# Background steps of a layer's FFN: issued by GpSimd through two buffers, one step at every hook, and spilled weight pairs as one transfer

## The chip, the cores and the metric

The kernel runs on one core of a Trainium2 chip. The metric is the device time of one execution in microseconds (us), lower is better. The engines of the core are named TensorE (PE; its weight loads are shown apart as PEld), VectorE (DVE), ScalarE (ACT), GpSimd (POOL) and SyncE (SP). SyncE and GpSimd can both start DMA transfers between the chip's main memory and the on-chip memory; each has a queue that it works off in order.

## What is computed

The reference is a trunk of two layers over a sequence of 1024 positions and 1024 channels, in fp32. Each layer has a token mixing and an FFN, both modulated by a vector `c`:

```python
for l in range(DEPTH):                       # DEPTH = 2
    mod = c_act @ w_ada[l] + b_ada[l]        # six vectors of 1024
    sh1, sc1, gt1, sh2, sc2, gt2 = jnp.split(mod, N_MOD, axis=-1)
    h = modulate(rms_norm(x, g_mix[l]), sh1, sc1)
    p = h @ w_in[l]                          # three head groups: Fourier, recurrence, attention
    ...
    x = x + gt1[:, None, :] * y
    h = modulate(rms_norm(x, g_ffn[l]), sh2, sc2)
    f = (silu(h @ w_ffn_gate[l]) * (h @ w_ffn_up[l])) @ w_ffn_down[l]   # 2816 inner channels
    x = x + gt2[:, None, :] * f
```

The change touches two things that layer 1 needs and that are made ready during layer 0's FFN: the products `c_act @ w_ada[1]`, and copies of layer 1's first weights.

## The kernel before

**Products.** A weight or an activation `w` is split into `hi` (rounded to the type that TensorE takes) and `lo = w - hi`, and every product is three matmuls, hi.hi, hi.lo and lo.hi (`mm3`). `split` makes the pair: ScalarE copies hi (line 199), VectorE subtracts (line 202). Nearly all operations are recorded at the line of their helper: 191 matmul, 199 activation, 202 tensor_tensor, 205 scalar_tensor_tensor.

**The FFN loop.** The 2816 inner channels are 22 blocks of 128, f = 0 to 21 (the first two run differently). For f from 2 on there are seven jobs (`p_job`, line 1363), each one operand of a fast scheme of products with 12 matmuls and half a weight; `after` (line 1399) takes their results from PSUM, applies silu and the product, and `a_split` writes the block's activations as a hi/lo pair into `ffa_A` (even f) or `ffb_A` (odd f), two halves each; the down weights go to `ffa_DW` and `ffb_DW`. In an even f eight `down_pair` (line 1463) are put in between, each 12 matmuls that multiply f-2 and f-1 by the down weights, and VectorE adds the result to the residual (line 205 on 128x1024). So TensorE needs the two `ffb_A` of an odd f right after the first down pair of the next even f has begun. A pair of f runs from the first down pair of one even f to that of the next.

**The order.** TensorE's order is written out by hand. `hook` (line 1471) is called twice in each job, 14 times in an f, and does what has to be done at that point. The order on VectorE, ScalarE, SyncE and GpSimd is set by a scheduler from the program; on the chip each of these engines takes its instructions in exactly that order and waits where one isn't ready.

**Background steps.** During layer 0's FFN, from f = 3 on, each hook also runs steps of a chain of generators (`bg`, line 356):

- `half_steps` (line 1521): 96 halves of `w_ada[1]`, 128x512 (256 KB) each. A step starts the load on SyncE (line 1527) into one raw buffer; the next step is one reduction on VectorE (line 1529, a product with `c` summed into one column, and the reading of the accumulator). 192 steps.
- `split_spill` (line 247): 26 pieces of weights of layer 1. A step loads a piece on SyncE (line 255), the next splits it into the one hi/lo pair of tiles at `M0`, the third stores hi and lo to main memory (`wspill`) with two transfers on SyncE (line 261). 78 steps.

```python
self.bg(1 if f % 2 or i < 3 or i > 10 else 2)
```

So an odd f runs 14 steps and an even one 22; the 270 steps reach to f = 18. In layer 1, `ready_load` (line 239) fetches such a spilled pair with two loads on GpSimd into one of three slots of the ring `WX` (set up in `mix`, line 1071).

Of the kernel before, what the change touches and what calls it, by code (L numbers as in the profile page):

```python
# [9 lines left out]
F32 = mybir.dt.float32  # L10
F32R = mybir.dt.float32r
AF = mybir.ActivationFunctionType
ALU = mybir.AluOpType
# [4 lines left out]
HALF = 512  # L18
# [7 lines left out]
U = 1024  # L26
# [34 lines left out]
for l in range(2):  # L61
# [10 lines left out]
               hi=[0, 1, 1, 1, 1, 0, 0, 0, 0, 0, 0, 1, 0, 1, 0],  # L72
# [58 lines left out]
class Trunk:  # L131
# [106 lines left out]

    def ready_load(self, i, n):
        def go():  # L240
            hi, lo = [a[:, :n] for a in self.WX()]
            self.nc.gpsimd.dma_start(out=hi, in_=self.ws[i, :, 0, :n])
            self.nc.gpsimd.dma_start(out=lo, in_=self.ws[i, :, 1, :n])
            return hi, lo
        return go

    def split_spill(self):
        l, h = 1, [self.M0, self.M0 + HALF]
        src = [(self.I["w_in"][l, t], U) for t in (T_G, T_G + 1, T_G + 2, T_K, T_Q)]
        src += [(self.I["dft"][c], U) for c in range(4)] + [(self.I["wv"][l, k], 768) for k in range(4)]  # L250
        raw = self.f(10 * U + HALF, HALF)
        for i, (w, n) in enumerate(src):
            for c in range(0, n, HALF):
                m = min(HALF, n - c)
                self.nc.sync.dma_start(out=raw[:, :m], in_=w[:, c:c + m])
                yield 1
                hi, lo = [self.f(o, m).bitcast(F32R) for o in h]
                self.split(raw[:, :m], hi, lo)
                yield 1
                for j, a in enumerate((hi, lo)):  # L260
                    self.nc.sync.dma_start(out=self.ws[i, :, j, c:c + m], in_=a.bitcast(F32))
                yield 1

    def pull(self):
        fn, w = self.queue.popleft()
# [619 lines left out]
    def slot(self, e, i, c0, n, p0=0, p1=P):  # L885
        o = (4 * e + i) * U + c0
        return self.QT[p0:p1, o:o + n]
# [183 lines left out]
    def mix(self, l, nb):  # L1071
        EN = mybir.EngineType
        self.SQ0, self.SQ, self.SK = self.X0 + 5 * U, self.X0 + 7 * U, 9 * U
        self.BI = Ring([10 * U, 10 * U + 1536, self.M0])
        self.w = self.M0 + 1536
        self.mr = Ring(20 * U + P + 4 * i for i in range(4))
        self.SB = Ring([4, 5, 6])
        self.bias = {}
        if l == 0:
            self.start()  # L1080
            self.raws = Ring([self.f(self.M0 + U, U)])
        else:
            self.ready.clear()
            self.weave(4, nb, TUNE["nb_m"])
            self.run(4)
            self.shut_ffn()
            wx = self.open("ready", WR1=(2 * U, F32R))
            slot = lambda a, o: (a[:, o:o + U], a[:, o + U:o + 2 * U])
            self.WX = Ring([slot(self.WR1, 0), slot(self.RA, 16 * U), slot(self.RA, 18 * U)])
            self.deep = 2  # L1090
        self.WR = Ring([8 * U, 10 * U])
        vp = self.open(f"v{l}", V=(8 * VW, F32R))
        lp = self.open(f"lru{l}", LW=(U, F32R), LF=(9 * U, F32))
        lru, fz = self.side(self.lru(l), WAITS[f"lru{l}"]), self.side(self.fourier_z(l), WAITS[f"fz{l}"])
        bg = self.side([lambda: next(self.steps)] * 30, WAITS["bg"]) if l == 0 else iter(())
        with self.tc.manual_schedule(engines={EN.Activation, EN.DVE, EN.Pool}):
            self.drive(2, fz, lru, bg)
            for _ in fz:
                pass
            self.drive(7 if l else 4, lru, bg)  # L1100
            self.WR = Ring([8 * U, self.X0 + 6 * U])
            self.drive(1, lru, bg)
            self.bias_load(l, 0, "s")
            self.attention_consts()
            def side():
                yield from lru
                self.shut(lp)
                self.qp = self.open(f"qk{l}", QT=(8 * U, F32R), PE=(4 * HALF, F32))
                self.PB = Ring(self.PE[:, i * HALF:(i + 1) * HALF] for i in range(3))
                self.EV = self.PE[:, 3 * HALF:]  # L1110
                self.slot_ones()
                yield from self.side(self.before_attention(l), WAITS[f"ba{l}"])
            side = side()
            self.drive(T_BIAS[l], side, bg)
            self.bias_load(l, 0, "t")
            self.drive(7 - T_BIAS[l], side, bg)
            if l:
                self.at = 16 * U
                self.deep = 1
            pt = self.at  # L1120
            wh = [o for o in self.WH.items if o != pt][0]
            self.PT = Ring([pt, pt + U])
            self.WH, self.WS = Ring([wh, wh + U]), HALF
            self.WR = Ring([8 * U, 8 * U + HALF])
            self.drive(1, side, bg)
            for _ in side:
                pass
            if l == 0:
                for _ in bg:
                    pass  # L1130
                self.steps = None
                self.mod_coef(0, 1)
            self.bias_load(l, 1, "s")
        with self.tc.manual_schedule(engines={EN.DVE}):
            early = self.mix_attention(l)
            self.WR = Ring((8 + i) * U for i in range(3))
            self.WH, self.WS = Ring([pt, wh]), U
            for _ in early:
                pass
        self.shut(self.qp)  # L1140
        self.shut(vp)
        if l:
            self.shut(wx)
# [327 lines left out]
    def hook(self, l, f):  # L1471
        if self.hf != f:
            self.hf, self.hi = f, 0
        i = self.hi
# [38 lines left out]
            self.late = None  # L1513
        if f > FIRST:
            if l == 0 and f == FIRST + 1 and i == 0:
                self.free.remove(self.M0)
                self.free.remove(self.M0 + HALF)
                self.c_spread()
            self.bg(1 if f % 2 or i < 3 or i > 10 else 2)

    def half_steps(self, seq):
        raw = self.f(10 * U + HALF, HALF)
        for l, c in seq:
            part = [self.mod[l] + 8 * c, self.tiny]
            for j in range(8):
                for i in range(2):
                    self.nc.sync.dma_start(out=raw, in_=self.I["ada"][l, 8 * c + j, :, i * HALF:i * HALF + HALF])
                    yield 1
                    self.nc.vector.tensor_tensor_reduce(  # L1529
                        out=raw, in0=raw, in1=self.f(self.M0 + i * HALF, HALF), op0=ALU.mult, op1=ALU.add,  # L1530
                        scale=1.0, scalar=0.0, accum_out=self.f(part[i] + j, 1))
                    yield 1
            m = self.f(part[0], 8)
            self.tt(m, m, self.v(l, V_ADA + 8 * c, 8), ALU.add)
            self.tt(m, m, self.f(self.tiny, 8), ALU.add)

    def ffn_jobs(self, l):
        for blk in range(4):
# [237 lines left out]
```

## Time and profile before

| | us |
|---|---|
| median of 3 runs | 2347.38 (2344.06 to 2350.89) |
| profiled execution | 2345.14 |
| its span on the core | 2343.4 |
| TensorE busy | 2219.9 (95% of the span) |
| VectorE busy | 1750.5 (75%) |
| ScalarE busy | 964.2 (41%) |
| GpSimd busy | 377.8 (16%) |

The profile's first part shows how long each engine was busy; with TensorE at 95% the time is TensorE's work and the gaps in it. Its granted clock over the span was 0.979 of the full one. The windows of the trace give the same numbers for one stretch; the waits say which engine stood still for which tile, and what it waited for; the timeline lists single instructions, with the idle time before each in brackets.

### The profile page before, as it was taken

The numbers are of one execution on the slowest core, as the hardware profiler recorded it, in microseconds if no ns is written. First come the engines' busy times: TensorE is split into PE (matmuls) and PEld (weight loads), VectorE is DVE, ScalarE is ACT, GpSimd is POOL, SyncE is SP. The second block draws the span as 40 slices with busy tenths as digits, with TensorE's granted clock in tenths as the row PEclk, the third lists the DMA queues.
The fourth block names the chain that finished last, engine by engine and source line by source line (L and its number), as shares of the span: only waits on it lengthen the run. The fifth ranks groups of instructions, "written<-read, shape, count | busy, mean of one in ns | idle before, by whom it ended". The sixth has DMA issues, their size and how long they took to land.

```text
span 2343.4 us, 27097 instructions
## 1 busy us (share of the span) xinstructions
PE 2219.9 (95%) x9802; PEld 1786.6 (76%) x9802; DVE 1750.5 (75%) x2840; ACT 964.2 (41%) x1608; POOL 377.8 (16%) x302
## 2 busy tenths in 40 slices
PE   6987998999999999999999999899999999999997
PEld 4765876778888887787777787678788888888886
DVE  8888689788788888776676456887876666666666
ACT  5365476444222222333244746745532222222223
POOL 4224276300000000000001445740000000000002
PEclk9997999989999999999999999999999999999998
DMA  8323423331333344465232262323021111111112
GB/s 299 103 67 111 133 82 121 109 118 46 102 121 115 121 124 121 135 201 171 66 133 76 69 195 69 106 80 113 28 63 54 55 54 54 55 52 48 55 37 77
DMA packets 91100, 230.53 MB, mean 98 GB/s; under 512 B 10451, under 2 KB 16083, under 8 KB 90966
## 3 DMA queue, kind: packets, MB, share of 16 engines
q1 hardware_dynamic: 82324, 194.42, 25.9%
q10 hardware_dynamic: 3746, 18.66, 2.3%
q0 software_dynamic: 4896, 15.73, 2.2%
q8 instruction: 77, 1.26, 0.2%
q14 instruction: 57, 0.47, 0.1%
HBM read 207.80 MB, written 20.97 MB: 98 GB/s over the span
## 4 chain that ended last, share of the span: by engine, by line
PE 64%; DVE 21%; DMA 7%; ACT 4%; issue 4%; POOL 1%; SPq 0%; ACTq 0%; DVEq 0%; POOLq 0%
PE psum L191 64%; DVE rounded L202 4%; DVE plain L202 3%; DMA plain<-in_ada 3%; DVE plain L205 2%; ACT plain L199 1%; DMA plain<-in_dft 1%; DVE plain L1529 1%; DVE psum L923 1%; DMA plain<-in_wv 1%; DVE psum L202 1%; DVE rounded L205 1%; DVE plain L341 1%; ACT lru_LF L199 1%; DVE lru_LF L725 1%
## 5 line engine op out<-in xcount | busy, mean ns | idle before, releaser
L191 PE MATMUL psum<-rounded 128*128 128x512 f32 (+2 forms) x4116 | 994.9, 391 | 20.8 <-DVE rounded L209 7.7
L191 PEld LDWEIGHTS psum<-rounded 128*128 128x128 f32 (+1 forms) x4116 | 771.5, 190 | 189.4 <-DVE rounded L209 11.5
L199 ACT ACTIVATE rounded<-plain 128x512 fp32r<-128x512 f32 (+4 forms) x404 | 263.8, 659 | 619.3 <-PE psum L191 472.1
L202 DVE TENSOR_TENSOR rounded<-plain,rounded 128x512 fp32r<-128x512 f32 (+4 forms) x410 | 317.8, 781 | 73.3 <-ACT rounded L199 70.1
L191 PE MATMUL psum<-hx_HX,rounded 128*128 128x512 f32 x1488 | 365.1, 392 | 1.9 <-DVE plain L202 1.9
L205 DVE SCALAR_TENSOR_TENSOR plain<-psum,plain 128x1024 f32<-128x1024 f32 (+2 forms) x256 | 269.9, 1062 | 111.5 <-PE psum L191 109.7
L191 PEld LDWEIGHTS psum<-hx_HX,rounded 128*128 128x128 f32 x1488 | 279.3, 188 | 63.9 <-ACT rounded L199 2.3
L191 PE MATMUL psum<-ffa_A,ffa_DW 128*128 128x512 f32 (+1 forms) x1080 | 299.8, 388 | 0.7 <-ACT plain L199 0.7
L191 PE MATMUL psum<-ffb_A,ffb_DW 128*128 128x512 f32 x960 | 275.0, 393 | 7.6 <-DVE ffb_A L202 4.3
L202 DVE TENSOR_TENSOR plain<-plain 128x512 f32<-128x512 f32 (+4 forms) x342 | 207.2, 617 | 73.1 <-DMA plain<-in_wu 41.2
L380 POOL TENSOR_TENSOR plain<-plain 128x512 f32<-128x512 f32 x6 | 8.1, 1357 | 1459.4 <-ACT plain L199 1459.4
L191 PEld LDWEIGHTS psum<-ffa_A,ffa_DW 128*128 128x128 f32 x1080 | 201.0, 188 | 43.9 <-ACT plain L199 1.5
L202 DVE TENSOR_TENSOR plain<-psum,plain 128x512 f32<-128x512 f32 (+1 forms) x288 | 193.4, 685 | 46.3 <-PE psum L191 42.5
L191 PEld LDWEIGHTS psum<-ffb_A,ffb_DW 128*128 128x128 f32 x960 | 179.7, 188 | 52.5 <-DVE ffb_A L202 8.6
L199 ACT ACTIVATE plain<-plain 128x512 f32<-128x512 f32 (+6 forms) x191 | 117.8, 629 | 152.2 <-DVE plain L202 76.7
L960 POOL TENSOR_TENSOR rounded<-qk_PE,rounded 128x512 fp32r<-128x512 f32 (+3 forms) x132 | 141.2, 1077 | 131.8 <-ACT rounded L199 107.6
L191 PE MATMUL psum<-rounded,v_V 128*65 128x512 f32 (+4 forms) x528 | 128.3, 357 | 14.5 <-ACT rounded L199 4.9
L191 PE MATMUL psum<-qk_QT 128*128 128x512 f32 (+8 forms) x432 | 107.7, 349 | 20.5 <-DVE plain L923 14.3
L191 PEld LDWEIGHTS psum<-rounded,v_V 128*65 128x65 f32 (+1 forms) x528 | 74.0, 149 | 52.2 <-POOL rounded L960 6.3
L202 DVE TENSOR_TENSOR psum<-psum,plain 128x256 f32<-128x256 f32 x240 | 97.7, 410 | 21.0 <-PE psum L191 14.3
L199 ACT ACTIVATE qk_PE<-psum 128x512 f32<-128x512 f32 (+4 forms) x168 | 83.4, 503 | 55.7 <-DVE psum L202 50.3
L199 ACT ACTIVATE ffa_DW<-plain 128x512 fp32r<-128x512 f32 x44 | 27.8, 631 | 186.0 <-PE psum L191 184.1
(140 smaller groups left out, 2138.2 us busy)
## 6 DMA issues: line engine op xcount, KB each, us to landing
plain<-in_ada SPq DMA_DIRECT2D x96, 256.0 KB, 2.6
plain<-in_wd SPq DMA_DIRECT2D x88, 256.0 KB, 2.6
plain<-in_wg SPq DMA_DIRECT2D x40, 512.0 KB, 3.6
plain<-in_wu SPq DMA_DIRECT2D x40, 512.0 KB, 3.6
plain<-in_ada SPq DMA_DIRECT2D x30, 512.0 KB, 3.5
wspill<-plain SPq DMA_DIRECT2D x44, 256.0 KB, 2.9
start_AT<-in_ada SPq DMA_DIRECT2D x18, 512.0 KB, 5.1
plain<-in_bias_t ACTq DMA_DIRECT2D x12, 768.0 KB, 4.6
```

Of the source, the lines that this page charges most:

```text
L191: self.nc.tensor.matmul(out=out, lhsT=lhsT, rhs=rhs, start=start, stop=stop)
L199: self.nc.scalar.activation(out=out, in_=in_, func=func, **kw)
L202: self.nc.vector.tensor_tensor(out=out, in0=a, in1=b, op=op)
L205: self.nc.vector.scalar_tensor_tensor(out=out, in0=a, scalar=s, in1=b, op0=op0, op1=op1)
L341: self.nc.vector.tensor_tensor_reduce(out=raw, in0=raw, in1=self.f(self.M0, U), op0=ALU.mult, op1=ALU.add, scale=1.0, scalar=0.0, accum_ou ...
L380: (self.nc.gpsimd if eng[m] else self.nc.vector).tensor_tensor(out=accs[i], in0=accs[i], in1=ss[i], op=ALU.add)
L725: nc.vector.tensor_tensor_scan(out=t, data0=a, data1=i, initial=0.0, op0=ALU.mult, op1=ALU.add)
L923: self.nc.vector.tensor_tensor_reduce(out=s, in0=s, in1=self.f(bo, a * w).rearrange("p (a b) -> p a b", a=a), op0=ALU.add, op1=ALU.max, sc ...
L960: (self.nc.vector if PLAN[self.l]["lo"][self.step] else self.nc.gpsimd).tensor_tensor(out=pl, in0=p, in1=ph.bitcast(F32), op=ALU.subtract)
L1529: self.nc.vector.tensor_tensor_reduce(out=raw, in0=raw, in1=self.f(self.M0 + i * HALF, HALF), op0=ALU.mult, op1=ALU.add, scale=1.0, scalar ...
```

## The change

- `half_steps` and `split_spill` use two raw buffers in turn, `raw2(0)` and `raw2(1)`. The second is one of the loop's 128x512 temporaries, taken for good at f = 3 (`self.r2`).
- All their loads and stores are issued by GpSimd and not by SyncE.
- The load of a piece is issued one step ahead: a step of `half_steps` starts the load of one half and reduces the half before; in `split_spill` a step starts a load, splits the piece before and stores it, and every second step is empty. The chain has 97 + 54 = 151 steps.
- `hook` runs one step each time, in odd and even f alike, so that the reductions run in f = 3 to 9 and the spill from f = 10 on.
- The hi/lo pair of a piece is stored with one transfer (128 x 2 x up to 512), and `ready_load` fetches a pair with one transfer; the slots of `WX` are whole tiles of 2U columns (U = 1024) for it.

```diff
--- before.py
+++ after.py
@@ -238,28 +238,30 @@
 
     def ready_load(self, i, n):
         def go():
-            hi, lo = [a[:, :n] for a in self.WX()]
-            self.nc.gpsimd.dma_start(out=hi, in_=self.ws[i, :, 0, :n])
-            self.nc.gpsimd.dma_start(out=lo, in_=self.ws[i, :, 1, :n])
-            return hi, lo
+            w = self.WX().rearrange("p (t n) -> p t n", t=2)[:, :, :n]
+            self.nc.gpsimd.dma_start(out=w, in_=self.ws[i, :, :, :n])
+            return w[:, 0], w[:, 1]
         return go
 
     def split_spill(self):
-        l, h = 1, [self.M0, self.M0 + HALF]
-        src = [(self.I["w_in"][l, t], U) for t in (T_G, T_G + 1, T_G + 2, T_K, T_Q)]
-        src += [(self.I["dft"][c], U) for c in range(4)] + [(self.I["wv"][l, k], 768) for k in range(4)]
-        raw = self.f(10 * U + HALF, HALF)
-        for i, (w, n) in enumerate(src):
-            for c in range(0, n, HALF):
-                m = min(HALF, n - c)
-                self.nc.sync.dma_start(out=raw[:, :m], in_=w[:, c:c + m])
-                yield 1
-                hi, lo = [self.f(o, m).bitcast(F32R) for o in h]
-                self.split(raw[:, :m], hi, lo)
-                yield 1
-                for j, a in enumerate((hi, lo)):
-                    self.nc.sync.dma_start(out=self.ws[i, :, j, c:c + m], in_=a.bitcast(F32))
-                yield 1
+        q, h = self.nc.gpsimd, self.f(self.M0, U).bitcast(F32R).rearrange("p (t n) -> p t n", t=2)
+        pieces = [(i, w, c, min(HALF, n - c)) for i, (w, n) in enumerate(self.spilled()) for c in range(0, n, HALF)]
+        for j, (i, w, c, m) in enumerate(pieces + [(0, None, 0, 0)]):
+            if w is not None:
+                q.dma_start(out=self.raw2(j)[:, :m], in_=w[:, c:c + m])
+            if j:
+                i, w, c, m = pieces[j - 1]
+                self.split(self.raw2(j - 1)[:, :m], h[:, 0, :m], h[:, 1, :m])
+                q.dma_start(out=self.ws[i, :, :, c:c + m], in_=h[:, :, :m].bitcast(F32))
+            yield 1
+            yield 1
+
+    def spilled(self):
+        src = [(self.I["w_in"][1, t], U) for t in (T_G, T_G + 1, T_G + 2, T_K, T_Q)]
+        return src + [(self.I["dft"][c], U) for c in range(4)] + [(self.I["wv"][1, k], 768) for k in range(4)]
+
+    def raw2(self, j):
+        return self.f((10 * U + HALF, self.r2)[j % 2], HALF)
 
     def pull(self):
         fn, w = self.queue.popleft()
@@ -1085,8 +1087,7 @@
             self.run(4)
             self.shut_ffn()
             wx = self.open("ready", WR1=(2 * U, F32R))
-            slot = lambda a, o: (a[:, o:o + U], a[:, o + U:o + 2 * U])
-            self.WX = Ring([slot(self.WR1, 0), slot(self.RA, 16 * U), slot(self.RA, 18 * U)])
+            self.WX = Ring([self.WR1, self.RA[:, 16 * U:18 * U], self.RA[:, 18 * U:20 * U]])
             self.deep = 2
         self.WR = Ring([8 * U, 10 * U])
         vp = self.open(f"v{l}", V=(8 * VW, F32R))
@@ -1513,26 +1514,28 @@
             self.late = None
         if f > FIRST:
             if l == 0 and f == FIRST + 1 and i == 0:
+                self.r2 = self.free.pop()
                 self.free.remove(self.M0)
                 self.free.remove(self.M0 + HALF)
                 self.c_spread()
-            self.bg(1 if f % 2 or i < 3 or i > 10 else 2)
+            self.bg(1)
 
     def half_steps(self, seq):
-        raw = self.f(10 * U + HALF, HALF)
-        for l, c in seq:
-            part = [self.mod[l] + 8 * c, self.tiny]
-            for j in range(8):
-                for i in range(2):
-                    self.nc.sync.dma_start(out=raw, in_=self.I["ada"][l, 8 * c + j, :, i * HALF:i * HALF + HALF])
-                    yield 1
-                    self.nc.vector.tensor_tensor_reduce(
-                        out=raw, in0=raw, in1=self.f(self.M0 + i * HALF, HALF), op0=ALU.mult, op1=ALU.add,
-                        scale=1.0, scalar=0.0, accum_out=self.f(part[i] + j, 1))
-                    yield 1
-            m = self.f(part[0], 8)
-            self.tt(m, m, self.v(l, V_ADA + 8 * c, 8), ALU.add)
-            self.tt(m, m, self.f(self.tiny, 8), ALU.add)
+        halves = [(l, c, j, i) for l, c in seq for j in range(8) for i in range(2)]
+        for q, (l, c, j, i) in enumerate(halves + [(0, 0, 0, 0)]):
+            if q < len(halves):
+                self.nc.gpsimd.dma_start(out=self.raw2(q), in_=self.I["ada"][l, 8 * c + j, :, i * HALF:i * HALF + HALF])
+            if q:
+                l, c, j, i = halves[q - 1]
+                part, raw = [self.mod[l] + 8 * c, self.tiny], self.raw2(q - 1)
+                self.nc.vector.tensor_tensor_reduce(
+                    out=raw, in0=raw, in1=self.f(self.M0 + i * HALF, HALF), op0=ALU.mult, op1=ALU.add,
+                    scale=1.0, scalar=0.0, accum_out=self.f(part[i] + j, 1))
+                if (j, i) == (7, 1):
+                    m = self.f(part[0], 8)
+                    self.tt(m, m, self.v(l, V_ADA + 8 * c, 8), ALU.add)
+                    self.tt(m, m, self.f(self.tiny, 8), ALU.add)
+            yield 1
 
     def ffn_jobs(self, l):
         for blk in range(4):
```

On VectorE in f = 5, from the evacuation (`plain<-psum,plain`) that follows the last result of f = 4, before; `L1529 ISA` is a reduction, and its second row, 128x1, the reading of its sum:

```order
L202 TENSOR_TENSOR plain<-psum,plain 128x512
L1529 ISA plain<-plain 128x512
L1529 ISA plain 128x1
L202 TENSOR_TENSOR plain<-psum,plain 128x512
L202 TENSOR_TENSOR rounded<-plain,rounded 128x512
L202 TENSOR_TENSOR plain<-psum,plain 128x512
L202 TENSOR_TENSOR rounded<-plain,rounded 128x512
L1529 ISA plain<-plain 128x512
L1529 ISA plain 128x1
```

The same place after (the reduction is now line 1531):

```order
L202 TENSOR_TENSOR plain<-psum,plain 128x512
L1531 ISA plain<-plain 128x512
L1531 ISA plain 128x1
L202 TENSOR_TENSOR plain<-psum,plain 128x512
L202 TENSOR_TENSOR plain<-plain 128x8
L1531 ISA plain<-plain 128x512
L1531 ISA plain 128x1
L202 TENSOR_TENSOR rounded<-plain,rounded 128x512
L202 TENSOR_TENSOR plain<-psum,plain 128x512
L202 TENSOR_TENSOR rounded<-plain,rounded 128x512
```

Two reductions stand before the second split result where there was one; to the end of the second `ffb_A` of this f there are ten where there were five, and as the other operations are 19 instead of 20, the row there holds 29 operations instead of 25.

On SyncE in the first pieces of the spill, before; `in_wg`, `in_wu` and `in_wd` are the loop's own weights, `in_w_in` a piece's load and `wspill` the stores of a hi and of a lo:

```order
L1306 DMA plain<-in_wg 128x1024
L255 DMA plain<-in_w_in 128x512
L1457 DMA plain<-in_wd 128x512
L261 DMA wspill<-plain 128x512
L1306 DMA plain<-in_wu 128x1024
L261 DMA wspill<-plain 128x512
L255 DMA plain<-in_w_in 128x512
L261 DMA wspill<-plain 128x512 x2
L255 DMA plain<-in_w_in 128x512
L261 DMA wspill<-plain 128x512 x2
```

On GpSimd after, from the first background load on (line 251 loads a piece, line 255 stores a pair):

```order
L1527 DMA plain<-in_ada 128x512 x95
L251 DMA plain<-in_w_in 128x512
L1527 DMA plain<-in_ada 128x512
L251 DMA plain<-in_w_in 128x512
L255 DMA wspill<-plain 256x1x512
L251 DMA plain<-in_w_in 128x512
```

The background transfers no longer stand between SyncE's weight loads; on GpSimd nothing else stands among them, each load comes before the store of the piece ahead of it, and a store is one transfer.

## Rows read from the trace of the kernel before

**Rows 1.** Windows of both FFN loops: us; PE, PEld, DVE, ACT, POOL busy; PEclk; DMA.
```profile
565.83:1177.58 611.75, 602.79 (x2611) 490.22 (x2610) 471.32 (x785) 182.75 (x305) 0.00 (x0) 1.00 0.41 127
1699.49:2297.30 597.81, 597.33 (x2612) 489.87 (x2611) 401.15 (x552) 166.81 (x276) 0.00 (x0) 1.00 0.16 52
```

**Rows 2.** Waits of TensorE in layer 0's loop: total us, times, longest.
```profile
PE psum L191 <- DVE ffb_A L202: 3.8, 8, 0.7
PE psum L191 <- ACT ffb_A L199: 3.2, 3, 2.2
```

**Rows 3.** Windows, columns as above: two pairs of layer 0, a spell, one of layer 1.
```profile
625.61:686.54 60.93, 60.72 (x266) 49.48 (x265) 49.91 (x92) 16.72 (x29) 0.00 (x0) 1.00 0.40 121
...
1054.78:1117.65 62.87, 60.97 (x265) 49.38 (x264) 43.72 (x65) 20.43 (x37) 0.00 (x0) 1.00 0.54 168
...
1122.18:1125.59 3.41, 3.41 (x9) 2.66 (x9) 0.36 (x2) 0.00 (x0) 0.00 (x0) 0.50 0.36 142
1759.25:1819.64 60.39, 60.39 (x265) 49.56 (x264) 40.69 (x56) 16.90 (x28) 0.00 (x0) 1.00 0.18 53
```

**Rows 4.** Waits of VectorE in layer 0's loop: total us, times, longest.
```profile
DVE plain L1529 <- DMA plain<-in_ada: 26.5, 37, 2.0
```

**Rows 5.** Timeline of VectorE, f = 3 and f = 5: start, duration, instruction, idle before.
```profile
610.24 0.69 DVE L1529 CUSTOM_DVE_ANT_0 plain<-plain 128x512 f32<-128x512 f32 x1 [2.50 <-ACT plain L199]
...
626.16 0.68 DVE L202 TENSOR_TENSOR ffb_A<-plain,ffb_A 128x512 fp32r<-128x512 f32 x1
...
670.25 0.69 DVE L202 TENSOR_TENSOR plain<-psum,plain 128x512 f32<-128x512 f32 x1 [1.31 <-PE psum L191]
671.75 0.69 DVE L1529 CUSTOM_DVE_ANT_0 plain<-plain 128x512 f32<-128x512 f32 x1 [0.81 <-DMA plain<-in_ada]
...
675.12 0.69 DVE L1529 CUSTOM_DVE_ANT_0 plain<-plain 128x512 f32<-128x512 f32 x1 [0.27 <-DMA plain<-in_ada]
...
685.96 0.68 DVE L1529 CUSTOM_DVE_ANT_0 plain<-plain 128x512 f32<-128x512 f32 x1
686.57 0.08 DVE L1529 DVE_READ_ACCUMULATOR2_ANT plain<- 128x1 f32 x1
...
687.17 0.68 DVE L202 TENSOR_TENSOR ffb_A<-plain,ffb_A 128x512 fp32r<-128x512 f32 x1
```

**Rows 6.** Timeline of layer 1 around the second `ffb_A` of an odd f.
```profile
1817.37 0.69 DVE L202 TENSOR_TENSOR ffb_A<-plain,ffb_A 128x512 fp32r<-128x512 f32 x1
...
1820.33 0.84 PE L191 MATMUL psum<-ffb_A,ffb_DW 128*128 128x512 f32 x3
```

**Rows 7.** Chain of waits in the spill, layer 0: start, us, what.
```profile
1033.44 0.64 ACT plain L199
1034.10 0.70 DVE plain L202
...
1066.86 0.64 ACT plain L199
```

**Rows 8.** Page, DMA issues: count, KB each, median us to landing.
```profile
plain<-in_ada SPq DMA_DIRECT2D x96, 256.0 KB, 2.6
...
plain<-in_wg SPq DMA_DIRECT2D x40, 512.0 KB, 3.6
...
rounded<-wspill POOLq DMA_DIRECT2D x12, 512.0 KB, 4.8
...
xspill<-plain SPq DMA_DIRECT2D x8, 512.0 KB, 2.9
```

**Rows 9.** GpSimd's loads of ready weights at layer 1's start: who waited; landing.
```profile
  ACT rounded L199: 7.6, 1
...
DMA to landing us min/median/max: 3.9/4.3/5.5
```

**Rows 10.** Timeline: GpSimd taking up an operation after ScalarE.
```profile
1184.79 2.61 ACT L199 ACTIVATE plain<-plain 128x512 f32<-128x512 f32 x4 [3.31 <-DVE plain L205]
...
1187.54 1.64 POOL L380 TENSOR_TENSOR plain<-plain 128x512 f32<-128x512 f32 x1 [739.11 <-ACT plain L199]
```

## Prediction

> **What bounds the kernel now.** I read the windows over the two FFN loops first, since the same ten pairs of f, from the first down products to the last, run in both and only layer 0's carries background work. In [rows 1] layer 0 takes 611.75 us and layer 1 takes 597.81. TensorE is busy for 602.79 and 597.33 of that, at a granted clock of 1.00, and VectorE for 471.32 and 401.15. Layer 1's loop is TensorE from end to end; layer 0's is that plus 13.94 us. **13.94 us is all that the loop can win**, however well the background is hidden, and 0.6% of 2347. The waits of TensorE [rows 2] name the larger pieces: eight waits for VectorE's write of `ffb_A` (3.8 us, the longest 0.7) and three for ScalarE's (3.2, one of 2.2). The rest is TensorE itself being longer: 60.72 us busy in a pair of f with reductions against 60.39 in a pair of layer 1 [rows 3], 0.33 a pair, and one spell of 3.41 us at a granted clock of 0.50, the lower of its two levels (1.2 GHz), behind the 2.2 us gap, which cost half of its length, 1.7 us. A pair with spill work at the end took 62.87.
>
> The third view is VectorE's. It takes its instructions in a fixed order, so a reduction whose half of `w_ada` has not landed holds up what is queued behind it: evacuations, splits, and the write of `ffb_A` that TensorE needs at once. It waited 37 times, 26.5 us, for `in_ada` [rows 4], nearly all of it free because VectorE has slack between two `ffb_A`. So the question is not how much the change moves off SyncE, but whether the two `ffb_A` of an odd f come earlier or later.
>
> **Part 1, the reductions.** The same 96 reductions are now packed into f = 3 to 9: 28 for each pair of f, where there were 18. Their own cost is VectorE time: in [rows 3] the pair with 18 has 49.91 us of VectorE and the pair without has 40.69, so 0.51 each, and a pair with 28 comes to 40.69 + 28 x 0.51 = 55.0 of 60.4 us. It fits, but with 5 us left instead of 10.
>
> What decides is the cycle of one buffer: reduction, wake-up of the queue, load, wake-up of VectorE. Before, two reductions on the single buffer lie 671.75 to 675.12, 3.37 us apart [rows 5]; the load takes 2.6 of that [rows 8], so 0.77 is reduction and wake-ups. GpSimd's wake-up is 0.14 (ScalarE ends at 1184.79 + 2.61, GpSimd starts at 1187.54, [rows 10]), some 0.08 more than what 0.77 leaves for SyncE (0.61 for the reduction, 0.16 for two wake-ups, so 0.08 each). So the new cycle is **C = L + 0.85**, with L the landing of a 256 KB load that GpSimd issues. No row shows one. SyncE's 256 KB land in 2.6 us and its 512 KB in 3.6; GpSimd's 512 KB take 4.8 in the middle [rows 8] and 3.9 at best [rows 9]. The excess over SyncE is thus 0.3 to 1.2 us and L is 2.9 to 3.8; without any excess, 2.6. I take 3.2, near the low end, because GpSimd's measured loads go out as twins and share the DMA engines, while these go out alone. C is 4.05.
>
> With two buffers the same buffer comes back every 5 or 6 VectorE operations in the new order. One operation takes 0.605 us (685.96 to 686.57 to 687.17, [rows 5]), so a buffer returns after 3.03 or 3.63 us. At C = 4.05 a return after 5 waits 1.02, and one after 6 waits 0.42. **f = 5:** from the evacuation at 670.25 to the end of the second `ffb_A` (687.17 + 0.68) before takes 17.6 us; the new order has 19 operations and 10 reductions there, 29 x 0.605 = 17.5. Without waits nothing changes; with them, two of 1.02 and three of 0.42 (the others are covered by the wait of the other buffer), it is 3.3 later. TensorE already waited some 0.4 there (eight waits in 3.8, [rows 2]), so 3.7. **f = 3:** from 610.24 to 626.16 + 0.68 before takes 16.6; now 30 operations, 18.2, and four returns at 0.42: 1.6 + 1.7 = 3.3 later, with the 0.4 again 3.7. **f = 7** has three reductions more in its stretch, some of them where VectorE idled: I take two waits, 0.9. **f = 9:** 0. That is 8.3 us of TensorE waiting. Two of these gaps (3.7) are longer than the one behind which the clock fell in [rows 3], so 2 x 1.7 = 3.4 more. Small change, 0.33 for each of the five pairs that still carry background: 1.7.
>
> A page speaks against GpSimd here: the Trainium skill, DMA: Bandwidth & Descriptors, Specifications, gives a first byte after about 1 us for loads that GpSimd issues and 0.6 for SyncE's, and its section "Issuing engine by pattern" puts simple loads on SyncE. An estimate from that page is L = 3.0, by which the sum would be some 2 us lower; the 0.3 to 1.2 us of [rows 8, 9] hold its 0.4, and no run here shows it for 256 KB.
>
> **Part 2, the spill.** 26 pieces: load, ScalarE copies hi, VectorE subtracts lo, store. Before, the single raw buffer sets the pace: seven ScalarE copies from 1033.44 to 1066.86 [rows 7], 5.57 us a piece. Now the next load is under way a step ahead, and the one pair of hi/lo tiles sets it: the copy of a piece waits until the store of the piece ahead has landed. The cycle is 0.64 + 0.70 [rows 7] + 0.14 wake-up + S + 0.26 for hand-overs (estimate). S, one 512 KB store by GpSimd, is not shown: SyncE's takes 2.9 [rows 8], with the same excess 3.2 to 4.1. I take 3.5: 5.24 us. In the new order the 26 pieces lie from the end of f = 9 to early f = 14, two pairs of 60.39 us and about 8, so 129 for 25 cycles; four narrow pieces are some 1.2 shorter. 25 x 5.24 - 4.8 = 126: it fits. Where it falls behind, `ffb_A` has 2.3 us to spare (VectorE done at 1817.37 + 0.69, TensorE at 1820.33, [rows 6]). I take 0.5. Queued behind a late hi copy are ScalarE's weight splits, and VectorE's lo behind them.
>
> **Part 3, what goes free.** GpSimd had no work in the loop (POOL 0.00 in [rows 1]), so nothing but the next background load stands behind a load that waits there. SyncE loses all of the background, and the weight loads no longer queue behind it. That can show only below the ceiling of 13.94. From f = 14 the loop should run like layer 1's.
>
> **Part 4, ready weights in layer 1.** One load instead of two twins; the first copy that needs them sees its data when all has landed, not half. GpSimd's twins landed in 4.3 us, and ScalarE waited for them once, 7.6 us [rows 9]; this is fetched ahead. I take 0, with 1 us either way.
>
> **Sum.** 8.3 + 3.4 + 1.7 + 0.5 = 13.9 us lost in the new loop, against 13.94 now: the same amount, in other places. The profiled execution is 2345.14 and the median of the runs 2347.38, 2.2 above it; the change carries no net term, so the forecast is **2347**.
>
> **Rivals.**
> *A, faster.* Alone on its queue GpSimd's load lands like SyncE's, L = 2.6, C = 3.45: returns after 6 fit, those after 5 wait 0.42. f = 3 is 1.6 + 0.4 late, f = 5 0.9 + 0.4, no clock falls: 3.3 + 1.7 = 5.0, a gain of 8.9, **2338**. For it: the excess is 0.3 at best. Against: 28 reductions with no slack in VectorE's order.
> *B, slower: the load's latency.* L = 3.8, C = 4.65: waits of 1.62 and 1.02. f = 3 is 1.6 + 4.1 + 0.4 = 6.1 late, f = 5 3.2 + 3.1 + 0.4 = 6.7, f = 7 and 9 about 3.6, together 16.4. Stores are as slow then (C below), 12; four falls of the clock 6.8; small change 1.7. 36.9 - 13.9 = +23, **2370**. It decides from L about 3.5 (C = 4.35), where the same steps give 13 + 3.4 + 1.7 + 3 = 21, +7.
> *C, slower: the chain of stores through the one pair.* Loads as in the forecast, but S = 4.1: a cycle of 5.84, 25 of them 146 - 4.8 = 141.2 against 129 and 2.3 to spare: 10 late, with one fall of the clock 11.7. 11.2 more than the forecast, **2358**. It decides from S about 3.9.
>
> **How the numbers follow.** Forecast 0.42, A 0.22, B 0.22, C 0.14. 0.3% is 7 us, about what a measurement of this kernel can tell from no change. Faster by more is A, 0.22; slower by more is B and C, 0.36; within it 0.42. The range takes in A, with L's lower bound, and C and most of B: 2337 to 2369.
>
> **What would show it.** The landing of the background loads on GpSimd's queue (3.2; at 2.6 A, from 3.5 B). VectorE's wait for `in_ada`, short and before nearly every reduction, with TensorE's waits for `ffb_A` at f = 4 and 6 at 3 to 4 us. Spells at half clock behind them. In f = 10 to 13 a ScalarE copy every 5.2 us, and no `ffb_A` waits over 1; pairs from f = 14 on at 60.4. The loop at 612 in all. It is wrong if the pairs of f = 4 to 8 are 60.5 each (A), or 63 to 67 (B), or if f = 12 and 14 are late by 5 (C), or if layer 1 moves by more than 1 us.

## The result

The changed kernel takes 2370.84 us (median of 5 runs, 2367.08 to 2372.71) against 2347.38: a ratio of 1.0095 (95% interval 1.0079 to 1.011), some 22 us slower. The forecast was no change, with a range that ended at 2369. Rival B's number, 2370, came nearest. Of its mechanism the late loads were right, and the late stores did not happen, as the runs below show.

The windows of the changed kernel (columns as in [rows 1]; layer 0's FFN loop, then its pairs of f from f = 4 on, then layer 1's loop):

```profile
566.79:1202.26 635.47, 613.25 (x2611) 497.20 (x2610) 474.08 (x785) 183.68 (x305) 84.44 (x148) 0.98 0.38 122
626.66:700.53 73.87, 65.80 (x266) 52.25 (x264) 61.17 (x128) 17.84 (x30) 17.42 (x33) 0.93 0.49 155
700.53:767.50 66.97, 63.92 (x265) 51.27 (x264) 55.41 (x112) 15.15 (x26) 14.73 (x28) 0.95 0.50 156
767.50:837.06 69.56, 63.76 (x265) 51.04 (x264) 57.06 (x115) 16.77 (x30) 15.12 (x28) 0.95 0.48 151
837.06:904.17 67.11, 63.31 (x266) 51.14 (x265) 53.92 (x83) 26.74 (x45) 14.79 (x24) 0.95 0.56 182
904.17:964.56 60.39, 60.39 (x265) 49.57 (x264) 44.53 (x66) 22.44 (x39) 14.98 (x24) 1.00 0.56 189
964.56:1026.57 62.01, 60.96 (x265) 49.48 (x264) 44.40 (x63) 18.90 (x33) 2.63 (x4) 1.00 0.27 88
...
1724.55:2322.36 597.81, 597.33 (x2611) 489.89 (x2610) 401.42 (x552) 166.70 (x276) 0.00 (x0) 1.00 0.17 52
```

Against [rows 1] the loop is 635.47 instead of 611.75, 23.7 longer, which is the whole loss; layer 1's loop is 597.81 in both. Of the 23.7, 10.5 is TensorE busy for longer (613.25 against 602.79) and 13.3 is TensorE standing still (22.2 against 9.0). It lies in four pairs, those that begin at f = 4, 6, 8 and 10. The first three hold 31, 27 and 29 reductions; the fourth holds only the last one, and begins with TensorE waiting for f = 9. Afterwards comes the spill, and its pairs are at 60.39 and 62.01, near the floor of 60.39.

The loop's first six pairs and its last four move in opposite directions. Before, then after:

```profile
565.83:930.58 364.75, 362.83 (x1580) 295.76 (x1579) 292.86 (x518) 102.68 (x171) 0.00 (x0) 1.00 0.38 116
930.58:1177.58 247.00, 239.96 (x1033) 194.46 (x1032) 178.46 (x268) 80.07 (x134) 0.00 (x0) 0.99 0.45 143
...
566.79:964.56 397.77, 376.59 (x1579) 303.55 (x1578) 314.40 (x567) 116.02 (x194) 81.81 (x144) 0.96 0.49 157
964.56:1202.26 237.70, 236.65 (x1033) 193.66 (x1032) 159.67 (x219) 67.66 (x111) 2.63 (x4) 1.00 0.21 65
```

The first six lose 33.0 us. The last four, in which the kernel before has its spill, win 9.3.

The waits in the loop, first of TensorE, then of VectorE (total us, times, longest):

```profile
PE psum L191 <- ACT ffb_A L199: 15.2, 5, 4.9
PE psum L191 <- DVE ffb_A L202: 3.2, 6, 0.8
PE psum L191 <- ACT rounded L199: 1.5, 1, 1.5
PE psum L191 <- DVE rounded L202: 1.3, 1, 1.3
...
DVE plain L1531 <- DMA plain<-in_ada: 27.6, 41, 3.1
```

TensorE waits for `ffb_A` as before, but five times for ScalarE's hi copy, with 15.2 us where [rows 2] had 3.2. ScalarE itself was waiting for VectorE, whose product feeds the copy; at f = 6 its row is this:

```profile
702.83 0.63 ACT L199 ACTIVATE ffb_A<-plain 128x512 fp32r<-128x512 f32 x1 [3.98 <-DVE plain L202]
```

VectorE's waits for `in_ada`, 27.6 us in 41, are hardly more than the 26.5 in 37 of [rows 4]; only they fall mostly into three pairs now, not six. In the pair 700.53 to 767.50 alone they are these:

```profile
DVE plain L1531 <- DMA plain<-in_ada: 8.0, 11, 1.9
DVE plain L205 <- PE psum L191: 2.7, 2, 1.6
DVE ffa_A L202 <- ACT ffa_A L199: 0.6, 1, 0.6
```

Busy time and waits of an engine always add up to about the whole pair, so the sum that tells something is another: VectorE's work and its waits for loads, set against the 60.39 us that TensorE alone needs for a pair. Here it is 55.41 + 8.0 = 63.4, so **VectorE has no slack left** and TensorE has to wait. Before, a pair of 60.93 held 49.91 us of VectorE's work ([rows 3]) and 3.4 us of such waits, 53.3 together, so the waits cost nearly nothing:

```profile
DVE plain L1529 <- DMA plain<-in_ada: 3.4, 5, 1.7
```

The second part of the loss is the clock. A pair at a mean granted clock of 0.95 spent a tenth of its time at 0.50 (1.2 GHz), since the other level is 1.00: the four pairs' 0.93 and three times 0.95 make about 31 us at half clock. TensorE was busy in some 26 us of them and so lost about 13 us, against 1.7 before. Each of the four pairs has a spell of 6.83 us at its first down products, where TensorE waits for `ffb_A` (the first of them at a wait of 4.9 us); three of the four:

```profile
631.95:638.78 6.83, 5.97 (x13) 4.40 (x14) 4.87 (x10) 1.09 (x2) 1.21 (x3) 0.50 0.51 148
771.90:778.73 6.83, 5.49 (x12) 4.02 (x13) 5.47 (x12) 1.89 (x3) 1.62 (x3) 0.50 0.58 183
840.17:847.00 6.83, 5.28 (x12) 3.85 (x13) 6.04 (x12) 1.89 (x3) 1.78 (x3) 0.50 0.42 128
```

### The profile page after: what moved, and what is told of

It reads as the page before. It is cut to its first block, busy times and chain, and to the rows that moved or that the text cites. A ratio compares the mean times of both kernels' runs of the same rounds, so it can differ in the third digit from the quotient of the medians.

```text
span 2370.9 us, 27017 instructions
## 1 busy us (share of the span) xinstructions
PE 2232.2 (94%) x9802; PEld 1796.1 (76%) x9802; DVE 1754.0 (74%) x2840; ACT 964.5 (41%) x1608; POOL 453.2 (19%) x433
## 4 chain that ended last, share of the span: by engine, by line
PE 52%; issue 20%; DVE 17%; DMA 4%; ACT 4%; POOL 3%; SPq 0%; POOLq 0%; ACTq 0%; DVEq 0%
PE psum L191 52%; DVE rounded L202 3%; POOL plain L1527 2%; DVE plain L202 2%; DMA wspill<-plain 1%; ACT plain L199 1%; DMA plain<-in_ada 1%; DVE plain L205 1%; DVE psum L925 1%; DVE psum L202 1%; DVE plain L343 1%; DVE rounded L205 1%; ACT lru_LF L199 1%; DVE start_AT L343 1%; ACT rounded L199 1%
## 5 line engine op out<-in xcount | busy, mean ns | idle before, releaser
L191 PE MATMUL psum<-ffb_A,ffb_DW 128*128 128x512 f32 x960 | 278.7, 398 | 18.9 <-ACT ffb_A L199 15.2
L202 DVE TENSOR_TENSOR plain<-plain 128x512 f32<-128x512 f32 (+5 forms) x342 | 209.7, 624 | 55.2 <-DMA plain<-in_wu 29.1
L199 ACT ACTIVATE plain<-plain 128x512 f32<-128x512 f32 (+7 forms) x191 | 117.8, 629 | 149.1 <-DVE plain L202 77.0
L1527 POOL DMA_DIRECT2D plain<-in_ada x96 | 52.0, 542 | 334.5 <-DVE plain L1531 175.0
```

The lines of the kernel that those rows point to most:

```text
L191: self.nc.tensor.matmul(out=out, lhsT=lhsT, rhs=rhs, start=start, stop=stop)
L199: self.nc.scalar.activation(out=out, in_=in_, func=func, **kw)
L202: self.nc.vector.tensor_tensor(out=out, in0=a, in1=b, op=op)
L1527: self.nc.gpsimd.dma_start(out=self.raw2(q), in_=self.I["ada"][l, 8 * c + j, :, i * HALF:i * HALF + HALF])
```

## The experiments

Ratios are to the kernel before, run on the same chip.

### The parts one by one

**Reductions alone.** The old `split_spill` is put back into the changed kernel:

```diff
     def split_spill(self):
...
-                q.dma_start(out=self.raw2(j)[:, :m], in_=w[:, c:c + m])
...
+                self.nc.sync.dma_start(out=raw[:, :m], in_=w[:, c:c + m])
+                yield 1
...
```

> The new reductions alone: two buffers, loads by GpSimd, one step at every hook; the spill stays as before (three steps a piece, one raw buffer, loads and stores on SyncE). Theory 1 (the loss is the reductions, 28 packed in a pair of f on VectorE): the four pairs from f = 4 to f = 10 take 67 to 74 us as with the whole change, and the time is 22 to 30 us above before, since the spill's own gain is missing. Theory 2 (the loss is GpSimd's stores and loads of the spill): within 5 us of before.

2370.03 us, ratio 1.0105 (1.0078 to 1.0132). The windows show the same four pairs:

```profile
627.65:704.15 76.50, 66.70 (x265) 52.65 (x264) 61.78 (x129) 17.84 (x30) 17.73 (x33) 0.91 0.46 151
704.15:771.00 66.85, 63.92 (x265) 51.69 (x264) 55.58 (x113) 15.50 (x26) 14.58 (x27) 0.95 0.49 154
```

The reductions are the whole loss. Theory 1 holds, theory 2 (the spill's stores) falls. The last four pairs of the loop take 237.63 us here, as short as with the whole change (237.70):

```profile
966.58:1204.21 237.63, 236.66 (x1033) 193.58 (x1032) 160.56 (x222) 68.96 (x114) 0.00 (x0) 1.00 0.22 68
```

So the 9.3 us that the change wins there come neither from putting the spill on GpSimd's queue nor from its two buffers or single store, which this run does not have. It shares with the whole change the one step at every hook and a spill that begins earlier in the loop.

**Spill alone.** `half_steps` and the steps at a hook as before, the rest as changed:

```diff
-            self.bg(1)
+            self.bg(1 if f % 2 or i < 3 or i > 10 else 2)
...
-        halves = [(l, c, j, i) for l, c in seq for j in range(8) for i in range(2)]
...
+        raw = self.f(10 * U + HALF, HALF)
...
```

> The new spill alone: two raw buffers, one store for a pair, GpSimd's queue; the reductions and the number of steps at a hook stay as before (one raw buffer, SyncE). Theory 1: the reductions cost what they cost before, and the spill pairs fall from 62 to 62.9 us to 60.4 to 62, so 2 to 6 us below before. Theory 2: 10 us or more above before.

2348.71 us, ratio 1.001 (0.9995 to 1.0024): no change. The 2 to 6 us that I expected to win did not come. The last pair with spill work got longer, not shorter (62.87 in [rows 3]):

```profile
1057.82:1124.73 66.91, 62.78 (x266) 50.57 (x264) 48.03 (x72) 22.72 (x42) 13.86 (x22) 0.97 0.48 161
```

This run keeps the old rate of steps, two at a hook in the middle of an even f. The four last pairs, which won 9.3 us with one step at every hook, win nothing here (247.66 us against 247.00). So it is the rate or the place of the steps that makes that gain; which of the two was not tried.

**Ready weights alone.** Only `ready_load` and the slots of `WX`:

```diff
-            self.nc.gpsimd.dma_start(out=hi, in_=self.ws[i, :, 0, :n])
-            self.nc.gpsimd.dma_start(out=lo, in_=self.ws[i, :, 1, :n])
...
+            self.nc.gpsimd.dma_start(out=w, in_=self.ws[i, :, :, :n])
...
```

> Only the fetch of a ready pair in layer 1 is one transfer instead of two. Both theories: within 2 us of before; layer 1's mixing, from the last down pair of layer 0 to the first of layer 1, moves by less than 1 us from 521.9.

2347.58 us, ratio 1.0005 (0.999 to 1.002), and 522.3 us from layer 0's last down pair to layer 1's first. Nothing, as expected.

### What of the reductions

**Fewer steps.** The whole change, with 5 steps in an odd f instead of 14:

```diff
-            self.bg(1)
+            if f % 2 == 0 or i in (0, 3, 6, 9, 12):
+                self.bg(1)
```

> The whole change, but an odd f runs 5 steps instead of 14 (an even one 14 as in the change), so 19 reductions a pair and none between the two writes of ffb_A from f = 5 on. Theory 1 (density): the pairs go back to 60.4 to 61, no spell at half clock behind the down pairs, and the time is 2336 to 2344. Theory 2 (the latency of GpSimd's queue, whatever the density): the pairs stay above 64 and the time above 2360.

2342.3 us, ratio 0.9979 (0.9964 to 0.9994): **faster than both kernels**, and the loop is 604.36 us, with 63.40 in one pair where I expected 60.4 to 61:

```profile
568.96:1173.32 604.36, 599.49 (x2612) 489.43 (x2610) 471.38 (x785) 182.39 (x305) 84.46 (x148) 1.00 0.40 129
689.92:753.32 63.40, 60.95 (x265) 49.48 (x264) 56.44 (x110) 18.49 (x32) 11.86 (x22) 1.00 0.46 146
753.32:813.83 60.51, 60.51 (x265) 49.49 (x264) 52.90 (x103) 16.18 (x28) 11.87 (x22) 1.00 0.47 148
```

The granted clock is 1.00 throughout. The 63.40 has a wait of 1.8 us for `ffb_A`. GpSimd's column counts its loads: 22 in a pair, not the 19 of my expectation. The pairs that the program gives 19 steps hold 22 or 23 reductions, as these run ahead of their place in it, so from here on I name runs by their steps and say what the trace holds.

Where the gain lies is seen in the two parts of the loop (first six pairs, last four):

```profile
568.96:936.78 367.82, 363.11 (x1579) 295.78 (x1578) 305.09 (x554) 107.58 (x181) 64.33 (x116) 1.00 0.45 144
936.78:1173.32 236.54, 236.38 (x1034) 193.65 (x1032) 166.29 (x232) 74.80 (x126) 20.12 (x32) 1.00 0.33 105
```

Against before, the first six pairs still lose 3.1 us and the last four win 10.5. The whole change wins nearly the same there; fewer steps only stop the reductions from eating it up.

**SyncE's loads at full density.**

```diff
-                self.nc.gpsimd.dma_start(out=self.raw2(q), in_=self.I["ada"][...])
+                self.nc.sync.dma_start(out=self.raw2(q), in_=self.I["ada"][...])
```

> The whole change, but SyncE issues the loads of the w_ada halves; two buffers and one step at every hook stay. Theory 2 (GpSimd's queue): its landing falls from 3.0 to about 2.6 us and the pairs go back to 61, 2340 to 2348. Theory 1 (reductions too dense for any queue of this latency): the cycle of a buffer falls by 0.4 us only, the pairs f = 4 to 10 still take 63 to 70, 2352 to 2372. A SyncE that waits for a buffer now also holds up the weight loads behind it.

2351.14 us, ratio 1.0017 (1.0 to 1.0035). Both theories had a part of it wrong: the queue alone takes back four fifths of the loss, though as many reductions stand in each pair. In the traced executions the loop is 610.47 us against 611.75 before, and another run whose loop is the one of before had 613.11; what this execution takes longer lies outside the loop. The load landed in 2.8 us, not 2.6, and VectorE's waits shrink from 27.6 us to 5.1. The pairs are at 62.4 to 64.9, where I expected 61 or 63 to 70:

```profile
692.16:755.34 63.18, 60.97 (x266) 49.48 (x265) 57.92 (x119) 17.00 (x28) 0.00 (x0) 1.00 0.54 171
...
DVE plain L1531 <- DMA plain<-in_ada: 5.1, 10, 1.2
...
plain<-in_ada SPq DMA_DIRECT2D x96, 256.0 KB, 2.8
```

**No loads at all.** Every reduction reads the first buffer, and all loads of `w_ada` but the first are left out, so this kernel's modulation of layer 1 is another:

```diff
-            if q < len(halves):
+            if q == 0:
...
-                part, raw = [self.mod[l] + 8 * c, self.tiny], self.raw2(q - 1)
+                part, raw = [self.mod[l] + 8 * c, self.tiny], self.raw2(0)
...
-                    out=raw, in0=raw,
+                    out=self.raw2(1), in0=raw,
```

> The whole change, but all w_ada loads save the first are left out (every reduction reads the same first buffer), so that VectorE never waits for in_ada; the 96 reductions stay on VectorE. If the loss is the waits for loads: pairs 60.4 to 61.5 and 2332 to 2342. If it is VectorE's own work, 28 reductions of 0.61 us in a pair: the pairs stay above 64 and the time above 2358. Half of each: 2345 to 2355.

2345.13 us, ratio 1.0 (0.9983 to 1.0018). The windows split what VectorE's own work costs from what the waits cost:

```profile
626.22:691.82 65.60, 62.58 (x265) 50.63 (x264) 63.32 (x134) 18.17 (x30) 0.00 (x0) 0.97 0.15 49
691.82:752.22 60.40, 60.40 (x266) 49.57 (x265) 59.40 (x124) 17.07 (x29) 0.00 (x0) 1.00 0.17 53
752.22:812.61 60.39, 60.39 (x266) 49.56 (x264) 56.67 (x110) 18.83 (x32) 3.58 (x6) 1.00 0.28 90
```

With nothing to wait for, VectorE works 59.40 us in a pair of 60.40 and TensorE never stands still: a full pair of reductions costs nothing by itself. The first pair is the exception: it holds 32 reductions and 63.32 us of VectorE's work, more than a pair's 60.39, and is 5.2 us late for that work alone. In the changed kernel that pair lost 13.5, the other three 6.6 to 9.2 each. The waits for loads, with the slow spells behind them, are thus the larger part, and in the three later pairs all of it. One thing is not separated: this run, the one before it and the half-sized loads below each have another order on VectorE than the changed kernel.

**As many steps, but in the even f.**

```diff
-            self.bg(1)
+            if f % 2 == 0 or i in (0, 2, 5, 7, 10, 12):
+                self.bg(1 if f % 2 or i < 3 or i > 10 else 2)
```

> The whole change with as many steps in a pair of f (28), but 6 in an odd f and 22 in an even one. If the number in a pair decides, the pairs stay at 66 to 70 and the time above 2362. If what decides is how many reductions stand ahead of the second ffb_A of an odd f (8, spread out, instead of 9 to 10, in clumps), the pairs fall to 61 to 64 and the time to 2342 to 2356.

2370.0 us, ratio 1.0098 (1.0061 to 1.0135).

```profile
697.05:763.85 66.80, 61.87 (x265) 49.09 (x264) 57.34 (x115) 16.88 (x30) 15.14 (x29) 1.00 0.49 158
763.85:831.62 67.77, 62.92 (x266) 50.47 (x264) 57.80 (x118) 16.86 (x30) 15.13 (x29) 0.97 0.48 155
```

The time is that of the whole change, so the number in a pair decides more than the place, and the account of my prediction, which looked only at the reductions ahead of the second `ffb_A` of an odd f, is not enough. The place is not nothing either. The four pairs that begin at f = 4 to 10 take 267.47 us together, against 277.51 in the changed kernel, and the next one gives most of that back: it has the spill, which this edit also packs into the even f, and takes 67.99 instead of 60.39.

**4 steps in an odd f, 16 in an even one.**

```diff
-            self.bg(1)
+            if f % 2 == 0 or i % 4 == 0:
+                self.bg(2 if f % 2 == 0 and i in (4, 8) else 1)
```

> As the run with 5 steps in an odd f, but 4 there and 16 in an even f (20 a pair). Theory 1: nothing stands between the two writes of ffb_A from f = 3 on, so the pairs are 60.4 to 61.5 and the time is within 3 us of that run (2339 to 2345). If the total of a pair matters more than the odd f, it is slower than that run.

2343.39 us, ratio 0.9991 (0.9974 to 1.0007). As expected within 3 us of the run with 5 steps; that it is faster than before is not shown. Its pairs with reductions are 60.9 to 62.6, not 60.4 to 61.5. The trace holds 22 or 23 reductions in each, as in the run with 5 steps, so this run does not test the number in a pair.

**24 steps a pair.** 10 in an odd f:

```diff
-            self.bg(1)
+            if f % 2 == 0 or i in (0, 1, 3, 4, 6, 7, 9, 10, 12, 13):
+                self.bg(1)
```

> The whole change with 10 steps in an odd f, 24 in a pair instead of 28. Theory 1 (one buffer's cycle with GpSimd, 4.6 to 4.7 us where VectorE waits, times the reductions of a pair over two buffers): 12 cycles are 55 to 56 us and fit into 60.4, 14 cycles are 64 to 66 and don't; so the loss mostly goes, the pairs are 61 to 64 and the time is 2342 to 2353. If the loss grows evenly with the number of steps (from -6 at 19 to +23 at 28): about +10, 2354 to 2360.

2357.12 us, ratio 1.0028 (1.0013 to 1.0043), or 6.6 us slower. I had put a threshold at the point where the cycles of the two buffers fill a pair, some 26 reductions; below it the loss should have nearly gone. The trace holds 26, 26 and 24 in the first three pairs, so two lie at the threshold and one just below it, and all three are 4 to 6 us late:

```profile
696.11:760.41 64.30, 62.01 (x265) 49.22 (x264) 54.68 (x109) 16.75 (x28) 14.04 (x26) 1.00 0.49 152
760.41:826.34 65.93, 62.76 (x266) 50.60 (x265) 56.09 (x112) 17.38 (x29) 12.94 (x24) 0.97 0.45 148
```

By steps in a pair the times are 19 (5 us faster), 24 (7 slower), 28 (22 slower); by reductions in the trace 22, some 26, and 27 to 31. The test of work plus waits for loads holds too. For the pair that begins at f = 6 it gives 53.7 us before (60.98 long), 59.4 without loads (60.40), 61.4 with 5 steps (63.40), 62.8 here (64.30) and 63.4 with the whole change (66.97). With SyncE's loads it is 60.2, and the pair is 63.18 all the same: VectorE's order is fixed, so slack that is there over a pair need not be there where a wait falls. That this is the reason was not tested.

**Half as many bytes.** GpSimd's loads at full density bring 256 of 512 columns, so the other half of each buffer is old data:

```diff
-                self.nc.gpsimd.dma_start(out=self.raw2(q), in_=...[:, i * HALF:i * HALF + HALF])
+                self.nc.gpsimd.dma_start(out=self.raw2(q)[:, o:o + n], in_=...[:, i * HALF + o:i * HALF + o + n])
```

> The whole change at full density, but each load by GpSimd brings 256 of the 512 columns (the other half of a buffer keeps older data, so layer 1's modulation comes out other). Landing falls from 3.0 to some 2.4 to 2.7 us, the cycle by 0.4 to 0.6. Theory 1 (the length of the cycle): the loss falls by half or more, 2345 to 2358. If it is GpSimd issuing at all (its work on descriptors, a lock against VectorE), whatever the landing: 2365 to 2373.

2362.41 us, ratio 1.0055 (1.0035 to 1.0076). The landing fell to 2.4 us, and VectorE's waits to about half:

```profile
plain<-in_ada POOLq DMA_DIRECT2D x94, 128.0 KB, 2.4
```

```profile
DVE plain L1533 <- DMA plain<-in_ada: 14.9, 26, 1.4
```

The loss fell by some 40% in time (in the traced loops by 55%, to 622.30 us), with no change to who issues; 2362.41 lies between my two ranges. So the length of the load is a cause; that it is the only thing that tells GpSimd from SyncE is not shown, because SyncE's run kept shorter waits (5.1 us) and some 9 us less by the two ratios. Their orders on VectorE differ too. This difference stays open.

**Fewer steps with SyncE's loads.** The last two edits together: 5 steps in an odd f, `w_ada` loads by SyncE.

> 5 steps in an odd f and 14 in an even one, with SyncE issuing the w_ada loads and GpSimd the spill. With a cycle of 3.5 us VectorE has room at 19 reductions a pair: its waits for in_ada fall below 10 us in all (21 with GpSimd), the pairs of f = 4 to 14 are 60.4 to 61.2, and the time is 2335 to 2341, 0.2 to 0.5% below before. If SyncE's weight loads are held up behind waiting background loads, waits for in_wu and in_wd show and the time is 2342 to 2348.

2346.53 us, ratio 0.9985 (0.997 to 0.9999). Not better than GpSimd at this density, and the waits did not fall:

```profile
DVE plain L1532 <- DMA plain<-in_ada: 21.3, 22, 2.6
```

There are fewer and longer waits (22, the longest 2.6 us) than with GpSimd at this density (33 in 21.1). Waits for `in_wu`, the sign of held-up weight loads, are 18.1 us against 16.0. The first six pairs are as long as GpSimd's, 367.68 us against 367.82, so at this density no difference between the queues is seen in them; the 5.3 us by which its loop is longer lie in the last four. Why SyncE kept the waits so short at full density and not here was not tried.

## Why the prediction was wrong

**The ceiling held.** 13.94 us was said to be all that the loop can win; the best version won 7.4 of it (611.75 to 604.36), and that with the last four pairs and not with the reductions.

**The load's landing was right, the cycle around it too short.** I took L = 3.2; the issues of the changed kernel on the page show 3.0 in the middle, and 3.2 for the store of a pair where I took S = 3.5:

```profile
plain<-in_ada POOLq DMA_DIRECT2D x96, 256.0 KB, 3.0
...
wspill<-plain POOLq DMA_DIRECT2D x22, 512.0 KB, 3.2
```

The page of the Trainium skill, DMA: Bandwidth & Descriptors, Specifications, was near on its point: its 0.4 us between the two ways to issue is the 0.4 between 3.0 here and the 2.6 of [rows 8], while at the same density SyncE's loads landed in 2.8 us and 0.2 is left. What I missed is the way from VectorE to the issue. One cycle of the changed kernel's timeline:

```profile
699.03 0.69 DVE L1531 CUSTOM_DVE_ANT_0 plain<-plain 128x512 f32<-128x512 f32 x1
699.65 0.08 DVE L1531 DVE_READ_ACCUMULATOR2_ANT plain<- 128x1 f32 x1
700.14 0.54 POOL L1527 DMA_DIRECT2D plain<-in_ada  x1 [0.87 <-DVE plain L1531]
...
703.05 0.69 DVE L1531 CUSTOM_DVE_ANT_0 plain<-plain 128x512 f32<-128x512 f32 x1 [0.26 <-DMA plain<-in_ada]
```

and one of before, whose next reduction is the 675.12 of [rows 5]:

```profile
672.37 0.08 DVE L1529 DVE_READ_ACCUMULATOR2_ANT plain<- 128x1 f32 x1
672.47 0.33 SPq L1527 DMA_DIRECT2D plain<-in_ada  x1
```

GpSimd starts its load 0.41 us after the accumulator was read (699.65 + 0.08 to 700.14), SyncE 0.02 us (672.37 + 0.08 to 672.47). I had taken GpSimd's 0.14 from [rows 10], which is the start of an arithmetic operation, not of a DMA. So the cycle is L + 1.13, not L + 0.85. And L isn't one number: it runs from 2.7 to 5.6, and VectorE waits more often for the slow ones. Over 40 reductions of f = 3 to 9 that waited, the landing is 3.55 on average and the cycle 4.7 instead of 4.05. That is rival B's cycle (4.65), reached with B's landing only now and then.

**The step that failed** is the one from the cycle to the time TensorE waits: 8.3 us by my account, while in the trace TensorE stood still for 22.2 us (9.0 before). Two things in it were wrong. The first is the cycle itself: the same rule of waits, at rival B's 4.65, gives 16.4. The second is that I laid the waits on single places: 3.3 us each in f = 3 and 5, 0.9 in f = 7, nothing in f = 9, as if the even f between them let VectorE catch up. My own numbers did not allow that. I had 55.0 us of VectorE's work in a pair of 60.4, 5 us to spare; waits at the rate that I had worked out for f = 5, 3.3 us for ten reductions, are 9 us in a pair with 28. The trace has 8 to 9 in each of the three pairs full of reductions, and these and the next are at 67 to 74. (The 55.0 was low as well: the pair of [rows 3] that I took for one with 18 reductions holds 16, which makes 0.58 us for each and 56.8 for 28.) TensorE waited 4.9, 2.1, 4.5 and 3.2 us for the hi copy of `ffb_A` at f = 4, 6, 8 and 10 (3.3, 3.3, 0.9 and 0 by my account), plus 2.8 for `rounded` weights that VectorE was late with inside f = 5, which I had not thought of. Even B's rule would have put too much on the first two places and too little on the last two.

**The clock was the other mis-sized term**: two spells, 3.4 us lost, against about 31 us at half clock, about 13 us lost. I took the length of a spell from the one of before (3.41), and each of the four pairs has one of 6.83.

**The spill was right.** A store every 5.0 us (929.37, 934.37, 939.41, 944.41 by GpSimd's timeline) against 5.24 by my sum, and it fits: 60.39 and 62.01 for its pairs. Rival C falls, and with it B's 12 us for the stores. That B's total came out is luck: its missing 12 was made good by the clock's 13 instead of 6.8 and by 22.2 us of standing still instead of 16.4. What the spill wins in the last four pairs, 9.3 us, no term of my sum had.

**Ready weights and layer 1**: 0, as said.

**Rival A** named the right question, GpSimd's latency against SyncE's, but even with SyncE's queue no gain is shown for the dense reductions (0 to 0.35% slower). What I never varied in my account is the density: the same buffers and queues with 5 steps in an odd f are 0.21% faster than before, because the reductions then leave standing what the last four pairs win.

## What to carry to other kernels

Ask of an engine off the critical path how much slack it has in one period, and set its work plus the waits for that work's own loads against it; here 3.4 us of waits were nearly free beside 50 us of work in 60, and 8 us beside 55 were not. Moving background work forward in time packs it more densely, and with a short buffer ring the round trip (wake-up, issue, landing, wake-up) then shows in every piece: the pace is a parameter to measure like a tile size. And where the matrix engine stands still, look at its granted clock behind the gap and add its slow spells to the price; here they cost about 13 us beside the 22 of standing still. Last, compare a change stretch by stretch: here a gain of 9 us was hidden behind a loss of 33.

## What the runs showed of the hardware

- GpSimd started a DMA 0.41 us after the VectorE instruction that it waited for; SyncE did in 0.02 to 0.03 us. With 0.2 to 0.4 us more to landing (3.0 against 2.8 at the same density, and 2.6 before), a round trip through GpSimd was some 0.6 to 0.8 us longer for 256 KB.
- No slowing of VectorE's instructions by GpSimd's issuing is seen: a reduction lasts 0.69 us in both kernels.
- Halving a GpSimd load from 256 to 128 KB took 0.6 us off its landing (3.0 to 2.4).
